# A hybrid encoder block: query latent by rows, later rotary angles, norm scales per token, and a new order at the last two norms

## The chip, the cores and the metric

The kernel runs on one core of one Trainium2 chip. The metric is the device time of one execution in microseconds, given as the median of several runs. One more execution is recorded by the hardware profiler; all the views below come from it.

The engines are named as the profile names them: PE multiplies matrices (PEld are its weight loads), DVE is the vector engine, ACT the scalar engine, POOL the GpSimd engine, SP the engine that issues most transfers. A "q" behind the name (SPq, ACTq) is the engine's own queue, which issues transfers. Every engine takes its instructions in the order in which they stand in its queue.

## The reference

The reference computes one layer for 256 tokens of 2048 features, all in float32:

```python
u = rms_norm(h, norm_pre_mix)
q_sb, k_sb, v_sb, q_lat, kv_lat, k_r, gate_logits = split(u @ w_in)
y_sb  = stick_breaking_attention(q_sb, k_sb, v_sb) @ w_o_sb          # 8 heads of 128
q     = rms_norm(q_lat, q_norm) @ w_uq                               # latent of 768
kv    = rms_norm(kv_lat, kv_norm) @ w_ukv                            # latent of 512
y_mla = mla_attention(q_nope, rope(q_rope), k_nope, rope(k_r), v) @ w_o_mla
g_sb, g_mla = sigmoid(gate_logits + b_gate)
h = h + rms_norm((g_sb * y_sb + g_mla * y_mla) @ w_out, norm_post_mix)
g, up = split(rms_norm(h, norm_pre_ffn) @ w_gate_up)                 # 5632 each
h = h + rms_norm((silu(g) * up) @ w_down, norm_post_ffn)
```

`rms_norm(x, g)` is x times the reciprocal root of its mean square over the features, times g. `rope` turns pairs of features by angles position x frequency; the positions are large (up to some 262,000), so the angle has to be reduced exactly before its sine is taken.

## The kernel before

**Products.** PE works with operands in a rounded float32 format. To keep float32 precision, each operand is split in two: `hi`, the rounded value, made on ACT, and `lo`, the rest, made on DVE. A product is then hi x hi + lo x hi + hi x lo. The activations are split once; the weights, nearly all of the 260 MB that are read, come once from memory and split on the way. One weight unit is a tile of 128 x 1024 (512 KB): SP issues its transfer into `raw`, ACT writes `hi` (L101), DVE writes `lo` (L102), and PE uses both. There are four buffers each of raw, hi and lo, so the splits can be up to four units ahead of PE.

**Stages, in order.** Feature-major products give features on the partitions and tokens along the free axis (`pair`): of the 512 columns of `xs[:, k]` the first 256 are hi of x, the others lo, so a weight tile's hi takes a 512-column product (L164) and its lo a 256-column one (L166); `fold` later adds the two halves. Token-major products (`token`, `two_products`) have 128 tokens on the partitions. The stages are: query latent (`lat_q`, three pairs of 128 features), key/value latent (`lat_kv`, two pairs), rope key (`kr`), `q_sb`, the products from the latents (`qn`, `qr`, `kn`, `vm`), `k_sb` and `v_sb` with the two attentions threaded in between, gates, the two output projections (`wo`), `wout`, the FFN's first product `gu` in eleven column blocks, and `wd`.

**The query latent before.** Each pair runs over all sixteen row tiles of x (four units of four row tiles) before the next pair starts. So the first pair takes x in as it goes: `load_first` loads and splits x's tiles between the cuts of the first four units (L115 on ACT, L116 on DVE).

**Hooks.** Small work is hung on weight units: `at_unit(u, fn)` runs `fn` when unit u's products have been written into the program. There its PE instructions are ordered behind that unit's last product, its ACT and DVE instructions behind the last split. The library's planner settles each engine's order, by its own costs, when the program is built; the engines then follow it. So a hook's product that waits for DVE holds up everything on PE behind it.

- `x_stats`: sums of squares of x, squares on ACT (L231), adds on POOL (L233), at units 3 to 11. `x_scale` (unit 18) makes from them the scale r0 of the first norm, once as a row over the tokens on all partitions (`row_sums`: a product with ones, L132) and once per token as a column (`col_sums`, L138).
- `angles`: the exact range reduction as a chain of some fifty DVE operations of 128 x 256 in eight steps, at units 5 to 12 (the last two of the ten hooks have nothing left).
- `lat_scale`: the scales of the two latents from their sums of squares (adds on POOL, L337 to L340), as rows for q and kv and a column for kv, at units 25, 29 and 32. `rsqrt` is a root on ACT and five operations on DVE; a row has 128 x 256 elements, a column 128 x 2.
- `take_k` and `rope_k`: the rope key's fold and rotation, at units 23 and 26.

**The last two norms.** `wout3` keeps its last four units apart by token half, so half 0 ends before half 1. `after_mix` (called at each half's end) takes squares (ACT), a reciprocal root (`neg_rsqrt`) and then four `residual`s of 128 x 512 on DVE (L721). `turned(t, n)` transposes one of them on PE (four transposes, L727), copies it on ACT (L730) and subtracts on DVE (L731) to get gu's operand `hs`. `gu0` runs its first six row tiles (HEAD0) for half 0, then for half 1, and the dictionary `turns` says before which product which turn is issued. Its first four weight units (AHEAD) are split by halves of 512 columns into slots of their own (L766, L767), written in the program behind the norm's work.

After `wd3`, `finish` does the same for the last norm: for each half the squares, the root, then out = fo x r3 + residual in four parts. Part 3 goes over ACT (L820) and POOL (L821) and is sent from ACT's queue, parts 0 to 2 over DVE (L823) and SP.

Of the kernel before, what the change touches and what calls it, by code (L numbers as in the profile page):

```python
# [10 lines left out]
F32 = mybir.dt.float32  # L11
# [6 lines left out]
P = 128  # L18
# [35 lines left out]
def block_kernel(ctx: ExitStack, tc: tile.TileContext, a: dict, out: bass.AP):  # L54
# [33 lines left out]
    def unit(stream, cols_n, cuts=1, first=None):  # L88
# [7 lines left out]
        for c in range(cuts):  # L96
            cs = slice(c * w, c * w + w)
            if first:
                first(c)
# [30 lines left out]
    def row_sums(acc, name):  # L130
        ps = at_bank(f"{name}_row")
        TE.matmul(ps[:, :T], lhsT=ones, rhs=acc, start=True, stop=True)  # L132
        return ps[:, :T]

    def col_sums(acc, name):
# [4 lines left out]
        return ps[:, 0:2]  # L140

# [12 lines left out]
    def pair(name, stream, K, per, rhs, first=None):  # L154
        ps = mm_pair(f"{name}_ps")
        for u in range(K // per):
            cuts = (4 if u == 0 else 2) if first else 1
            hi, lo = unit(stream, per * 2 * P, cuts, first and (lambda c: first(u, c)))
# [53 lines left out]
    def load_first(u, c):  # L212
        if u == 0:
            load_x(c, 1)
        else:
            load_x(4 * u + 2 * c, 2)

    r0 = const.tile([P, T], F32, tag="r", name="r0")
    r0c = const.tile([P, 2], F32, tag="r0c", name="r0c")
    r0q_krr, r0_sq, trig = slot("r0q_krr"), slot("r0_sq"), slot("trig")  # L220
# [18 lines left out]
    def x_scale():  # L239
        acc = acc_x[0]  # L240
        v = slot("vx")[:, 0]
# [3 lines left out]
        V.tensor_scalar(vc, col_sums(acc, "x"), 1.0 / D, EPS, op0=ALU.mult, op1=ALU.add)  # L245
        rsqrt(r0c, vc)
        V.tensor_tensor(r0_sq[:, 0], r0, r0, op=ALU.mult)
        V.tensor_tensor(r0c_sq, r0c, r0c, op=ALU.mult)
        V.tensor_scalar_mul(r0q, r0, SB_SCALE)
# [75 lines left out]
    lat = {}  # L325
    for nm, n in (("q", 6), ("kv", 4)):
        acc = slot(f"acc_{nm}")[:, 0]
        g = cols[f"{nm}_norm"]
        for p in range(n // 2):
            first = nm == "q" and p == 0  # L330
            ps = pair(f"lat_{nm}{p}", "w_lat", KD, 4, xk, load_first if first else None)
            s = tmp.tile([P, 2, T], F32, tag="t2", name="s", bufs=6)
            fold(ps, None, s)
# [14 lines left out]
        lat[nm] = acc  # L348

# [26 lines left out]
    at_unit(count[0] + 1, take_k)  # L376
# [26 lines left out]
    at_unit(26, rope_k)  # L403
# [4 lines left out]
    def lat_scale(r, sums, acc, r_x, r_x_sq, n, name, scale=None):  # L408
        v = slot(f"v_{name}").rearrange("p a b -> p (a b)")[:, :r.free_size()]
# [499 lines left out]
```

## Time and profile before

| | us |
|---|---|
| runs shown: median (lowest to highest) | 1394.03 (1393.38 to 1395.98) |
| the profiled execution's own time | 1395.33 |
| its span, first to last instruction | 1393.6 |
| first product of `lat_q` | 4.69 |
| first of `lat_kv`, of `kr`, of `q_sb` | 46.70, 70.81, 76.45 |
| first of `gate`, of `wo`, of `wout` | 278.37, 468.09, 558.03 |
| first of `gu`, of `wd` | 648.87, 1143.77 |
| end of the last product | 1384.48 |

How to read the lines of the profile: a line of the timeline has start, duration, engine, line of the kernel, operation, output<-inputs, shapes, and in brackets the idle time of the engine before it and what ended it. A line of groups ends in "| busy us, mean ns of one | idle time before, by what ended it". A line of the waits has the total in us, the number of waits and the longest one. A product's duration is longer than the time to the next one's start, as products overlap on PE; its cost in a row of them is from start to start. A true float32 product (not the rounded format) appears as two instructions.

### The profile page before, as it was taken

What the parts mean: (1) busy time and instruction counts of PE and PEld (TensorE: products, weight loads), DVE (VectorE), ACT (ScalarE), POOL (GpSimd) and SP (SyncE); (2) the same over time, 40 slices, a digit from 0 to 9 for tenths busy, and PEclk for the clock granted to TensorE, in tenths of its full rate; (3) what the DMA queues carried; (4) which work ended last, traced back from release to release, by engine and by line L of the source; (5) the groups of instructions that cost most, each with busy time, mean ns of one, the idle gap of its engine ahead of it and who ended that gap; (6) DMA issues with size and microseconds to landing.
All of it is one profiled execution on the core that took longest, in us unless ns stands there. A gap on an engine that the chain in (4) does not pass through costs nothing.

```text
span 1393.6 us, 16788 instructions
## 1 busy us (share of the span) xinstructions
PE 1373.6 (99%) x6400; PEld 1141.1 (82%) x6400; DVE 804.1 (58%) x927; ACT 681.1 (49%) x816; POOL 59.2 (4%) x89
## 2 busy tenths in 40 slices
PE   7999999999999999999999999999999999999997
PEld 6888888888888888887888888888888888888886
DVE  7997966555555566557555545555455555444444
ACT  7564454466548443445644444444444454434343
POOL 3210000000002100000000000000000001000001
PEclk9999999999999999999999999999999999999999
DMA  7565655455567766664766666665656666666663
GB/s 239 186 207 164 199 167 166 153 182 183 172 209 250 219 184 190 185 196 121 218 190 184 192 186 193 184 191 185 195 185 192 184 207 205 192 196 195 195 188 116
DMA packets 74977, 262.88 MB, mean 189 GB/s; under 512 B 8592, under 2 KB 9744, under 8 KB 74768
## 3 DMA queue, kind: packets, MB, share of 16 engines
q1 hardware_dynamic: 72720, 254.86, 58.8%
q0 software_dynamic: 1744, 6.29, 1.4%
q8 instruction: 50, 0.82, 0.2%
q10 hardware_dynamic: 432, 0.66, 0.1%
q14 instruction: 31, 0.25, 0.0%
HBM read 259.68 MB, written 2.10 MB: 188 GB/s over the span
## 4 chain that ended last, share of the span: by engine, by line
PE 94%; DVE 3%; DMA 1%; ACT 1%; issue 1%; SPq 0%; POOL 0%; DVEq 0%; ACTq 0%
PE gu_ps L629 11%; PE gu_ps L631 11%; PE gu_ps L630 11%; PE wd_ps L200 6%; PE wd_ps L202 6%; PE wd_ps L201 6%; PE gate_ps L202 4%; PE gate_ps L200 4%; PE gate_ps L201 4%; PE k_sb_ps L164 2%; PE q_sb_ps L164 2%; PE wout_ps L200 2%; PE wout_ps L202 2%; PE wo_ps L631 2%; PE wo_ps L630 2%; PE wo_ps L629 2%
## 5 line engine op out<-in xcount | busy, mean ns | idle before, releaser
L773 DVE SCALAR_TENSOR_TENSOR lo_w_gu<-raw_w_gu,packed,hi_w_gu 128x1024 fp32r<-128x1024 f32 x172 | 221.0, 1285 | 213.3 <-ACT hi_w_gu L772 211.6
L772 ACT ACTIVATE hi_w_gu<-raw_w_gu,packed 128x1024 fp32r<-128x1024 f32 x172 | 198.0, 1152 | 230.4 <-PE gu_ps L630 226.4
L629 PE MATMUL gu_ps<-hi_w_gu,hs 128*128 128x512 f32 x704 | 276.6, 393 | 0.9 <-ACT hi_w_gu L766 0.9
L631 PE MATMUL gu_ps<-lo_w_gu,hs 128*128 128x512 f32 x704 | 275.1, 391 | 0.7 <-DVE lo_w_gu L767 0.7
L630 PE MATMUL gu_ps<-hi_w_gu,hs 128*128 128x512 f32 x704 | 273.5, 389 | 0.0
L102 DVE TENSOR_TENSOR lo_w_down<-raw_w_down,hi_w_down 128x1024 fp32r<-128x1024 f32 x88 | 109.2, 1242 | 120.4 <-ACT hi_w_down L101 120.1
L101 ACT ACTIVATE hi_w_down<-raw_w_down 128x1024 fp32r<-128x1024 f32 x88 | 93.3, 1061 | 135.6 <-PE wd_ps L201 127.4
L629 PEld LDWEIGHTS gu_ps<-hi_w_gu,hs 128*128 128x128 f32 x704 | 132.2, 188 | 31.2 <-ACT hi_w_gu L766 2.3
L631 PEld LDWEIGHTS gu_ps<-lo_w_gu,hs 128*128 128x128 f32 x704 | 132.1, 188 | 28.7 <-DVE lo_w_gu L767 1.4
L630 PEld LDWEIGHTS gu_ps<-hi_w_gu,hs 128*128 128x128 f32 x704 | 132.2, 188 | 27.1
L102 DVE TENSOR_TENSOR lo_w_gate<-raw_w_gate,hi_w_gate 128x1024 fp32r<-128x1024 f32 x64 | 78.7, 1234 | 70.1 <-ACT hi_w_gate L101 63.8
L200 PE MATMUL gate_ps<-hi_w_gate,xs 128*128 128x512 f32 x256 | 100.6, 393 | 0.0
L202 PE MATMUL gate_ps<-lo_w_gate,xs 128*128 128x512 f32 x256 | 99.7, 390 | 0.0
L201 PE MATMUL gate_ps<-hi_w_gate,xs 128*128 128x512 f32 x256 | 99.6, 389 | 0.0
L101 ACT ACTIVATE hi_w_gate<-raw_w_gate 128x1024 fp32r<-128x1024 f32 x64 | 67.4, 1055 | 62.0 <-PE gate_ps L201 53.7
L102 DVE TENSOR_TENSOR lo_w_out<-raw_w_out,hi_w_out 128x1024 fp32r<-128x1024 f32 x32 | 39.2, 1226 | 38.8 <-ACT hi_w_out L101 38.6
L101 ACT ACTIVATE hi_w_o<-raw_w_o 128x1024 fp32r<-128x1024 f32 x32 | 34.0, 1061 | 51.7 <-PE wo_ps L630 45.2
L102 DVE TENSOR_TENSOR lo_w_o<-raw_w_o,hi_w_o 128x1024 fp32r<-128x1024 f32 x32 | 39.2, 1225 | 32.0 <-ACT hi_w_o L101 31.4
L101 ACT ACTIVATE hi_w_out<-raw_w_out 128x1024 fp32r<-128x1024 f32 x32 | 34.0, 1061 | 47.2 <-PE wout_ps L201 36.3
L202 PEld LDWEIGHTS gate_ps<-lo_w_gate,xs 128*128 128x128 f32 x256 | 48.0, 188 | 10.1
L201 PEld LDWEIGHTS gate_ps<-hi_w_gate,xs 128*128 128x128 f32 x256 | 48.1, 188 | 9.7
L200 PEld LDWEIGHTS gate_ps<-hi_w_gate,xs 128*128 128x128 f32 x256 | 48.1, 188 | 9.6
(447 smaller groups left out, 2557.0 us busy)
## 6 DMA issues: line engine op xcount, KB each, us to landing
raw_w_gu<-in_w_gu SPq DMA_DIRECT2D x176, 512.0 KB, 3.6
raw_w_down<-in_w_down SPq DMA_DIRECT2D x88, 512.0 KB, 3.5
raw_w_gate<-in_w_gate SPq DMA_DIRECT2D x64, 512.0 KB, 3.6
raw_w_o<-in_w_o SPq DMA_DIRECT2D x32, 512.0 KB, 3.8
raw_w_out<-in_w_out SPq DMA_DIRECT2D x32, 512.0 KB, 3.5
raw_w_lat<-in_w_lat SPq DMA_DIRECT2D x16, 512.0 KB, 4.8
raw_w_q<-in_w_q SPq DMA_DIRECT2D x16, 512.0 KB, 4.0
raw_w_k<-in_w_k SPq DMA_DIRECT2D x16, 512.0 KB, 3.8
```

Of the source, the lines that this page charges most:

```text
L101: split_ins[0] = S.activation(hi[:, cs], raw[:, cs], AF.Copy)
L102: split_ins[1] = V.tensor_tensor(lo[:, cs], raw[:, cs], hi[:, cs].bitcast(F32), op=ALU.subtract)
L164: TE.matmul(ps[:, j, :], lhsT=hi[:, o:o + P], rhs=r, start=k == 0, stop=False, skip_group_check=True)
L200: TE.matmul(ps[t], lhsT=l[0][:, ts], rhs=hi[:, cs], start=k == 0, stop=False)
L201: TE.matmul(ps[t], lhsT=l[1][:, ts], rhs=hi[:, cs], start=False, stop=False)
L202: mm = TE.matmul(ps[t], lhsT=l[0][:, ts], rhs=lo[:, cs], start=False, stop=k == K - 1)
L629: TE.matmul(ps[t][:, j], lhsT=x[0][:, ts], rhs=hi[j], start=k == 0, stop=False)
L630: TE.matmul(ps[t][:, j], lhsT=x[1][:, ts], rhs=hi[j], start=False, stop=False)
L631: mm = TE.matmul(ps[t][:, j], lhsT=x[0][:, ts], rhs=lo[j], start=False, stop=k == K - 1)
L772: split_ins[0] = S.activation(hi, raw, AF.Copy, scale=g)
L773: split_ins[1] = V.scalar_tensor_tensor(lo, raw, g, hi.bitcast(F32), op0=ALU.mult, op1=ALU.subtract)
```

## The change

- **Query latent.** The weight stream of the query latent is laid out by rows: one unit is one row tile with all 768 columns (sixteen units of 384 KB instead of twelve of 512 KB), and the three pairs are computed side by side in six accumulators, the row tile outermost. x's tiles are loaded one by one (from the fifth on two by two) ahead of the unit that needs them. The first two units are cut in three. The last two row tiles are run pair by pair, so that the pairs end one after the other. Units are numbered anew: four more lie ahead of everything behind the query latent.
- **Angles.** The same eight steps at units 17, 19, 21, 24, 26, 28, 31 and 32 (ten hooks again). The statistics of x are at units 2 to 17; `rope_k` is at unit 40.
- **Scales.** All three are made per token as columns of two; `spread` multiplies the ones matrix by each column (DVE) and, at a later unit, turns it into a row by a product with the identity (PE), copied out on ACT. x's sums are at unit 22 with the spread at 26, q's at 27 and 33, kv's at 30 and 36. `row_sums` is gone.
- **Norm before the FFN.** gu0's first four weight units are issued at units 11, 14, 19 and 22 of the 24 of wout0 to wout2. `after_mix` issues two residuals per half, and `later_residuals` the other four behind the turn (1, 0). The turns stand in a new order. The FFN's squares on ACT come behind the second half's root.
- **Last norm.** POOL has no part in it. For half 0 all four parts go over DVE and SP. For half 1, part 3 is made on PE: the identity times the residual plus a diagonal of r3 times fo, copied out on ACT and sent from ACT's queue.

```diff
+    def spread(col, name, u, *rows):
+        b = const.tile([P, 2, P], F32, tag="spread", name=f"{name}_b", bufs=2)
+        for t in range(2):
+            V.tensor_scalar_mul(b[:, t], ones, col[:, t:t + 1])
+        def rest():
+            ps = at_bank(f"{name}_row")
+            for t in range(2):
+                TE.matmul(ps[:, t * P:t * P + P], lhsT=b[:, t], rhs=ident, start=t == 0, stop=True, ...)
+            for row, factor in rows:
+                S.activation(row, ps[:, :T], AF.Copy, scale=factor)
+        at_unit(u, rest)
...
     def x_scale():
-        V.tensor_scalar(v, row_sums(acc, "x"), 1.0 / D, EPS, op0=ALU.mult, op1=ALU.add)
-        rsqrt(r0, v)
...
+        spread(r0c, "r0", 26, (r0, 1.0), (r0q, SB_SCALE))
...
-    for u in range(3, 12):
+    for u in [*range(2, 17, 2), 17]:
         at_unit(u, lambda: next(stat_steps, None))
-    at_unit(18, x_scale)
-    for u in [*range(5, 14), 16]:
+    at_unit(22, x_scale)
+    for u in (17, 19, 21, 24, 26, 28, 31, 32, 34, 37):
         at_unit(u, lambda: next(trig_steps, None))
...
+    def first_products():
+        both = [mm_pair(f"lat_q{p}_ps") for p in range(2)]
+        ps = [[b[:, j] for j in range(2)] for b in both] + [[at_bank(f"lat_q2{j}_ps") for j in range(2)]]
+        order = [(k, p) for k in range(KD - 2) for p in range(3)]
+        order += [(k, p) for p in range(3) for k in range(KD - 2, KD)]
+        w = {}
+        for k, p in order:
+            if k not in w:
+                if k < 4:
+                    load_x(k, 1)
+                elif k % 2 == 0:
+                    load_x(k, 2)
+                w[k] = unit("w_lat", 768, 3 if k < 2 else 1)
+            hi, lo = w[k]
+            for j in range(2):
+                o = (2 * p + j) * P
+                TE.matmul(ps[p][j], lhsT=hi[:, o:o + P], rhs=xs[:, k], ...)
+                mm = TE.matmul(ps[p][j][:, 0:T], lhsT=lo[:, o:o + P], rhs=xs[:, k, 0], ...)
+            if p == 2:
+                unit_done(mm)
+            if k == KD - 1:
+                yield ps[p]
...
-    at_unit(25, lambda: lat_scale(rq, row_sums, lat["q"], r0, r0_sq[:, 0], 768, "q", MLA_SCALE))
-    at_unit(29, lambda: lat_scale(rkv, row_sums, lat["kv"], r0, r0_sq[:, 0], 512, "kv"))
-    at_unit(32, lambda: lat_scale(rkvc, col_sums, lat["kv"], r0c, r0c_sq, 512, "kvc"))
+    at_unit(27, lambda: lat_scale(rqc, "q", 768, 33, rq, MLA_SCALE))
+    at_unit(30, lambda: lat_scale(rkvc, "kv", 512, 36, rkv, 1.0))
...
     def after_mix(ps, t):
         squares(ss1, ps, t, 3)
         r1s[t] = neg_rsqrt(ss1, t, "r1", lambda: mg_part(ps, t, 3))
+        roots.append(ready[0][0])
         with tc.issue_after(ready[0][1]):
-            for n in range(4):
+            for n in range(2):
                 residual(t, n)
...
+    def later_residuals():
+        with tc.issue_after(last_turn[0]):
+            for n in range(2, 4):
+                for t in range(2):
+                    residual(t, n)
...
+    for k in range(AHEAD):
+        at_unit(count[0] + (11, 14, 19, 22)[k], lambda k=k: first_units.update({k: up_unit(0, k)}))
...
     def ffn_squares(t):
-        for n in range(4):
-            squares(ss2, hres[t, n], t, n)
+        with tc.issue_after(roots[1]):
+            for n in range(4):
+                squares(ss2, hres[t, n], t, n)
...
+        with tc.issue_after(first_residual[k >= HEAD0]):
+            return up_unit(c, k)
...
-    turns = {(0, 0): (1,), (0, 2): (2,), (0, 4): (3,), (1, 0): (0, 1), (1, 3): (2,), (1, 6): (3,)}
+    steps = {(0, 0): [(turned, 0, 1)], (0, 5): [(turned, 1, 0), (later_residuals,)], (1, 0): [(turned, 1, 1)],
+             (1, 2): [(turned, 0, 2)], (1, 3): [(turned, 1, 2)], (1, 4): [(turned, 0, 3)], (1, 5): [(turned, 1, 3)]}
...
     def finish(ps, t):
         squares(ss3, ps, t, 3)
+        if t == 1:
+            last = at_bank("last")
+            TE.matmul(last, lhsT=ident, rhs=hres[t, 3], start=True, stop=False)
         r3 = neg_rsqrt(ss3, t, "r3", lambda: fo_part(ps, t, 3))
-        for n in (3, 0, 1, 2):
+        if t == 1:
+            diag = const.tile([P, P], F32, tag="diag", name="diag")
+            V.tensor_scalar_mul(diag, ident, r3)
+            TE.matmul(last, lhsT=diag, rhs=fo[t, 3], start=False, stop=True)
+        for n in range(4):
             o = fo[t, n]
-            if n == 3:
-                S.activation(o, o, AF.Copy, scale=r3)
-                G.tensor_tensor(o, o, hres[t, n], op=ALU.add)
+            if t == 1 and n == 3:
+                S.activation(o, last, AF.Copy)
             else:
                 V.scalar_tensor_tensor(o, o, r3, hres[t, n], op0=ALU.mult, op1=ALU.add)
-            (S if n == 3 else nc.sync).dma_start(out[...], o)
+            (S if t == 1 and n == 3 else nc.sync).dma_start(out[...], o)
```

More of the change, by code (lines that the diff above doesn't have):

```diff
@@ L152, in unit_done, with pair @@
                 fn()
[L154 removed]
+    def pair(name, stream, K, per, rhs):
         ps = mm_pair(f"{name}_ps")
         for u in range(K // per):
[L157 to L158 removed]
+            hi, lo = unit(stream, per * 2 * P)
             for i in range(per):
```

108 lines of the change are left out of this document (57 added, 51 removed).

## The prediction

> **What bounds the kernel now.** I read the page's busy shares first, then PE's waits, then the timelines of the three places where PE isn't back to back: the start, the turn from the output projection to the FFN, and the tail.
>
> ```profile
> span 1393.6 us, 16788 instructions
> PE 1373.6 (99%) x6400; PEld 1141.1 (82%) x6400; DVE 804.1 (58%) x927; ACT 681.1 (49%) x816; POOL 59.2 (4%) x89
> ```
>
> PE is the bound, so only idle or slow PE time can be won; the change leaves the big products alone. PE's waits name the places:
>
> ```profile
> PE lat_q_ps L164 <- DVE xs L116: 4.7, 1, 4.7
> PE lat_q_ps L166 <- DVE lo_w_lat L102: 2.6, 5, 1.0
> PE lat_q_ps L164 <- ACT hi_w_lat L101: 1.2, 1, 1.2
> PE gu_ps L629 <- ACT hi_w_gu L766: 0.9, 2, 0.7
> PE gu_ps L631 <- DVE lo_w_gu L767: 0.7, 2, 0.4
> PE lat_kv_ps L166 <- DVE lo_w_lat L102: 0.4, 1, 0.4
> ```
>
> The 4.7 us are the first load; the next two rows (3.8 us) lie in the query latent, two in gu0, one in the key/value latent.
>
> **Part 1, query latent by rows.** PE's timeline, start to start:
>
> ```profile
> 4.69 0.77 PE L164 MATMUL lat_q_ps<-xs,hi_w_lat 128*128 128x512 f32 x1 [4.69 <-DVE xs L116]
> 6.11 0.63 PE L164 MATMUL lat_q_ps<-xs,hi_w_lat 128*128 128x512 f32 x1
> 6.75 0.63 PE L164 MATMUL lat_q_ps<-xs,hi_w_lat 128*128 128x512 f32 x1
> 11.68 0.50 PE L164 MATMUL lat_q_ps<-xs,hi_w_lat 128*128 128x512 f32 x1 [1.16 <-ACT hi_w_lat L101]
> 46.70 0.40 PE L164 MATMUL lat_kv_ps<-xs,hi_w_lat 128*128 128x512 f32 x1
> 47.05 0.40 PE L164 MATMUL lat_kv_ps<-xs,hi_w_lat 128*128 128x512 f32 x1
> ```
>
> A hi/lo pair takes 0.64 us early (6.11 to 6.75) and 0.35 later (46.70 to 47.05), though the granted clock of the windows below reads 1.00 in both. The 96 pairs of the query latent need 96 x 0.35 = 33.6; they took 46.70 - 4.69 = 42.0. So 8.4 us go to the slow start and the stalls. Before, the first quarter of the pairs needs all sixteen row tiles of x; now row tile k brings six pairs, 2.1 us of PE, for one x tile and one weight tile of 768 columns. When are these there?
>
> ```profile
> 8.37 0.42 ACT L101 ACTIVATE hi_w_lat<-raw_w_lat 128x256 fp32r<-128x256 f32 x1 [0.83 <-DMA raw_w_lat<-in_w_lat]
> 10.99 0.63 ACT L101 ACTIVATE hi_w_lat<-raw_w_lat 128x512 fp32r<-128x512 f32 x1 [1.02 <-DMA raw_w_lat<-in_w_lat]
> 8.00:11.00 3.00, 2.52 (x8) 1.36 (x6) 1.36 (x4) 1.33 (x4) 0.00 (x0) 1.00 0.81 224
> 11.00:14.00 3.00, 2.10 (x10) 1.52 (x11) 2.17 (x4) 2.49 (x6) 0.00 (x0) 1.00 0.99 343
> L101 ACT ACTIVATE hi_w_uqn<-raw_w_uqn 128x768 fp32r<-128x768 f32 x8 | 6.8, 847 | 10.9 <-PE q_sb_ps L164 5.7 <-PE qn_ps L164 4.0 <-issue 1.2
> L102 DVE TENSOR_TENSOR lo_w_uqn<-raw_w_uqn,hi_w_uqn 128x768 fp32r<-128x768 f32 x8 | 7.7, 957 | 7.4 <-ACT hi_w_uqn L101 7.4
> ```
>
> The windows' last columns are the granted clock, DMA share and GB/s. Before, eight 128 KB pieces had landed at 8.37 and 1.57 MB at 10.99. The new order also starts with eight 128 KB pieces (tiles 0 and 1), so PE starts at 4.69 as now; tile 2 completes 1.57 MB: at 10.99 at the latest, or 8.37 + 0.52 MB at 343 GB/s = 9.9 with its longer rows. Splitting 768 columns costs 0.85 + 0.96, so tile 2 can run at 11.7 to 12.8; I take 12.2. PE's first twelve pairs end near then: slow up to about 11 (the change of pace lies before 11.68), (11 - 4.69) / 0.64 = 9.9 pairs, and 2.1 more at 0.35 reach 11.7. Then 14 tiles x 6 x 0.351 = 29.5: the latent ends at 41.7 instead of 46.70, 5.0 less. Later tiles need 0.52 MB in 2.1 us, 249 GB/s, under the 343; DVE per tile is 0.96 + 0.48, ACT no more. One late tile more would cost 1 us: 4.9 won, 3.5 to 5.5.
>
> The rows show 343 GB/s with 256 KB transfers, several in flight. The Trainium skill (DMA: Bandwidth & Descriptors, section Bandwidth) asks for transfers of 1 MiB and gives 0.68 us for 4 KB and 6.15 for 1 MB. An estimate from that page, one transfer after the other, makes 4.1 us of a 384 KB and a 128 KB piece, and this part a loss of some 20 us; the trace speaks against it, and the sum goes by the trace.
>
> **Part 2, angles and scales.** The angles move from units 5 to 13 (in the query latent) to 17 to 37, behind it; the latents' folds of q now come in one lump there; the three 256-wide rsqrt chains become two-column ones.
>
> ```profile
> 47.00:79.00 32.00, 30.96 (x62) 1.00 0.55 165
> L345 DVE SCALAR_TENSOR_TENSOR lat_q<-s,packed,lat_q 128x256 fp32r<-128x256 f32 x6 | 5.6, 948 | 0.2 <-ACT lat_q L344 0.2
> L345 DVE SCALAR_TENSOR_TENSOR lat_kv<-s,packed,lat_kv 128x256 fp32r<-128x256 f32 x4 | 1.8, 480 | 0.0
> L124 DVE RECIPROCAL r<-r 128x256 f32<-128x256 f32 x1 | 1.8, 1754 | 0.0
> 42.91 4.36 POOL L233 TENSOR_TENSOR ssx<-ssx,sq 128x512 f32<-128x512 f32 x3
> ```
>
> The first row is DVE alone, busy and its count: 30.96 of 32 us. DVE is full where PE hardly waits yet, so here the gain can be given back. The stretch from 47 to 79 (key/value latent, rope key, first unit of q_sb) keeps its PE work. Its DVE work changes by: the row chain out, about 1.75 + three ops like the 0.4 us ones, -2.9; folds of two more q pairs, each one 0.6 us operation and two of the 0.48 row, which overlap to 1.4, +2.8; the angles, 9.2 before and 9.6 now by their ops of 0.28 and 0.42; and more adds on POOL beside it, some six more of about 0.9. An add slows DVE: 0.95 instead of 0.48 in the rows; half of their 5.7 us is +2.9, bounds 0 and 5.7. Together +3.2. Against it stand two units split ahead (2 x 1.2), as DVE has 2.1 us per 1.44 of work in the new query latent. Net +0.8 on PE, from -0.4 (today's wait goes too) to +3.6.
>
> PE also gets three spread products and one column product more in place of three row products. A row product is 0.43 (67.16 to 67.59) and two 128-column products of the same type are as long; the added column product is 67.59 to 67.95 and a slower restart: 0.45.
>
> ```profile
> 67.16 0.59 PE L132 MATMUL x_row<-ssx,ones 128*128 128x256 f32 x2
> 67.59 0.50 PE L138 MATMUL x_col<-ones,ssx 128*128 128x1 f32 x4
> 67.95 0.47 PE L164 MATMUL lat_kv_ps<-xs,hi_w_lat 128*128 128x512 f32 x1
> 82.73 0.15 DVE L248 TENSOR_TENSOR r0c_sq<-r0c 128x2 f32<-128x2 f32 x1
> ```
>
> A new wait: PE, in order, stands at unit 26 for the spread operand that DVE makes from r0c. Before, r0c took 82.73 - 67.95 = 14.8 from the sums, 2.9 of it the row chain's; now units 23 to 26 give it 4 x 2.8 + 0.4 = 11.7. It just fits: 0, at most 3, and it is the same backlog as above. Behind it would stand q_sb's products. Units 27 to 33 and 30 to 36 leave six units, 17 us: nothing. Angles and rope_k land by unit 40, needed after 50. Part 2 costs 0.8 + 0.45 = 1.25.
>
> **Part 3, gu0.** Four weight units are now loaded and split between units of wout1 and wout2, where ACT and DVE have room; only two residuals of each half come before the first turn.
>
> ```profile
> 644.91 0.60 PE L727 MATMUL tp<-ident,x 128*128 128x128 f32 x4
> 645.26 0.48 PE L200 MATMUL wout_ps<-hi_w_out,mixed3h 128*128 128x512 f32 x1
> 646.74 1.47 PE L727 MATMUL tp<-ident,x 128*128 128x128 f32 x12
> 648.87 0.50 PE L629 MATMUL gu_ps<-hi_w_gu,hs 128*128 128x512 f32 x1 [0.65 <-ACT hi_w_gu L766]
> 662.62 0.50 PE L629 MATMUL gu_ps<-hi_w_gu,hs 128*128 128x512 f32 x1
> 650.51 2.73 DVE L721 SCALAR_TENSOR_TENSOR x<-mg,r,x 128x512 f32<-128x512 f32 x4
> ```
>
> From 646.74 to 662.62, 15.9 us, PE does 28 transposes and 39 products. (The stretch's groups count 14, 13 and 12 products by line, the first of the next three among them and one unrecorded.) A clean group of four transposes takes 0.35 (644.91 to 645.26) and some 0.1 of restart (that product lasts 0.48, one in mid-stream 0.39); a product is 0.227 after the one before it (three in 0.68). So 7 x 0.45 + 39 x 0.227 = 12.0, and 3.9 can be won. What is late next is the second half's residual, 650.51 to 653.2 for all four and near 652 for the two that now come first, against its turn on PE at 646.74 + 0.45 + 5 x 6 x 0.227 = 654.0; the four late residuals follow (4 x 0.68) and the first of their turns stands on PE at 658.6, two units into the second half. If four splits in wout cost PE something, it is the 12 products of a unit (2.7 us) against DVE's 1.23 + 1.48: level, with four buffers of lead. I take 3.4, 2.0 to 3.9.
>
> **Part 4, tail.**
>
> ```profile
> 1384.09 0.39 PE L202 MATMUL wd_ps<-lo_w_down,hid10h 128*128 128x512 f32 x1
> 1384.56 0.35 ACTq L824 DMA_DIRECT2D out_h<-fin  x1
> 1384.96 0.60 ACT L687 ACTIVATE sqo<-wd_ps 128x512 f32<-128x512 f32 x1 [2.27 <-POOL fin L821]
> 1387.04 3.08 DVE L823 SCALAR_TENSOR_TENSOR fin<-fin,r,x 128x512 f32<-128x512 f32 x3
> 1387.84 1.73 POOL L821 TENSOR_TENSOR fin<-fin,x 128x512 f32<-128x512 f32 x1 [3.31 <-ACT fin L820]
> ```
>
> PE ends at 1384.48, but ACT's queue holds the squares behind an output transfer that waits for POOL: 0.45 lost. Without POOL the three last DVE products take 3 x 0.68 (the residuals' row, the same instruction) = 2.05, not 3.08; the diagonal, 128 wide, lies between the 0.15 of a two-column operation and the 0.48 of a 256-wide one: 0.2, ahead of them. Gain 0.45 + 1.0 - 0.2 = 1.25. The fourth part goes over PE (0.86, twice a 256-column product of that type), ACT (0.6, the squares' shape) and ACT's queue, ready beside the third. The opening product of that pair, on the residual, lies in the 2.5 us that r3 takes. Two output transfers closer together cost some 0.15. 1.1, from 0.6 to 1.6.
>
> **Sum.** -4.9 + 1.25 - 3.4 - 1.1 = -8.2 (bounds: -10 to -3). The profiled execution took 1395.33 (span 1393.6), 1.3 over the median 1394.03 of the runs; 1387.1 by the one, 1385.8 by the other. Medians are compared: 1386.
>
> **Rivals.**
> - DVE takes the start back (+4.9 instead of +0.8 in units 17 to 28): for it, DVE at 97%; against it, 0.4 us of waits there now. 1390.
> - gu0 is bound by the residuals and turns, not by the weights: part 3 gives 0.5. For it, ACT makes the turns' copies between the splits; against it, both named waits are on w_gu. 1389. Both rivals at once: 1393, no change.
> - Slower: each POOL add holds DVE for its whole 1.45 us (4.36 / 3) in units 17 to 26. That is 11.1 us of adds instead of the 2.9 counted, 8.2 more, and r0c's chain, behind that, makes PE wait its 3 us at the spread: -8.2 + 8.2 + 3.1 = +3.1, 1397. It decides from 11 us of backlog. Against it: 0.95, not 1.9, for L345.
>
> The Trainium skill (SBUF — State Buffer, section Who interferes with whom) says that a DVE instruction with two SBUF inputs and a GpSimd one that reads SBUF fully block each other, the later waiting; by that rule the last rival, 1397. The trace shows only part of such waits.
>
> **Chances.** Forecast 0.62 (own range 1383 to 1389), DVE 0.14, gu0 0.10, both 0.06, slower 0.08. Under 0.2% (2.8 us) a measurement can't tell from no change. Faster: 0.62 + 0.10 + most of 0.14 = 0.83; same 0.09; slower 0.08. The range 1382 to 1391 leaves out the last two cases and some edges.
>
> **What would show it.** Right: the key/value latent starts near 42; its span stays within 24 to 25 us; no PE wait at the spread; gu0's first product within 1 us of wout's last, with no wait on w_gu, and its first 39 products over in 12 to 13 us; the last squares within 0.1 us of PE's end and no POOL in the tail. Wrong: waits of PE on lo_w_lat, lo_w_kr, lo_w_q or the spread operand over 3 us in all; waits on the turned rows in gu0; slower products anywhere else.

## The result and the profile after

| | before | after |
|---|---|---|
| median of the runs side by side (lowest to highest) | 1394.32 (1393.38 to 1395.98) | 1387.47 (1386.74 to 1387.83) |
| the profiled execution, its span | 1395.33, 1393.6 | 1387.83, 1386.1 |
| first product of the key/value latent, of `kr`, of `q_sb` | 46.70, 70.81, 76.45 | 42.42, 65.47, 71.14 |
| first product behind `q_sb` (q/k norms) | 122.81 | 119.88 |
| last product of `wout`, first of `gu` | 646.51, 648.87 | 643.82, 644.41 |
| first product of `wd`, last of `wd`, end | 1143.77, 1384.09, 1393.60 | 1137.06, 1377.38, 1386.13 |

The ratio is 0.9949, with a 95% interval of 0.9932 to 0.9966: 6.9 us faster by the medians, 7.5 by the two spans. The forecast was 1386.0. Cut at the stages of the table, the spans' 7.5 us come from: query latent -4.4 (and 0.1 later at the start); from there to the end of `q_sb`, +1.35; small shifts over attention, gate and wo, +0.2; turn to the FFN, -4.0; tail, -0.8.

The waits of PE in the changed kernel (engine, tile and line, what ended the wait; total, count, longest):

```profile
PE lat_q_ps L342 <- DVE xs L114: 4.8, 1, 4.8
PE last L878 <- DVE diag L877: 1.6, 1, 1.6
PE lat_q_ps L342 <- ACT hi_w_lat L99: 1.3, 1, 1.3
PE r_row L144 <- DVE r_b L139: 1.2, 1, 1.2
PE lat_q_ps L343 <- DVE lo_w_lat L100: 0.5, 1, 0.5
```

The first load stays. The five waits on `lo_w_lat` in the query latent have become one pair of waits at one tile; `w_gu` is gone from the list. New are the wait at the spread, which the prediction had put at nothing, and one in the tail. The timeline of PE shows where these stand:

```profile
10.36 0.28 PE L343 MATMUL lat_q_ps<-xs,lo_w_lat 128*128 128x256 f32 x1
11.91 0.50 PE L342 MATMUL lat_q_ps<-xs,hi_w_lat 128*128 128x512 f32 x1 [1.27 <-ACT hi_w_lat L99]
12.91 0.39 PE L343 MATMUL lat_q_ps<-xs,lo_w_lat 128*128 128x256 f32 x1 [0.49 <-DVE lo_w_lat L100]
...
42.42 0.40 PE L172 MATMUL lat_kv_ps<-xs,hi_w_lat 128*128 128x512 f32 x1
...
75.28 0.71 PE L144 MATMUL r_row<-ident,r_b 128*128 128x128 f32 x4 [1.16 <-DVE r_b L139]
...
643.82 0.40 PE L210 MATMUL wout_ps<-lo_w_out,mixed3h 128*128 128x512 f32 x1
644.06 0.60 PE L759 MATMUL tp<-ident,x 128*128 128x128 f32 x4
644.41 0.48 PE L659 MATMUL gu_ps<-hi_w_gu,hs 128*128 128x512 f32 x1
...
654.55 0.39 PE L659 MATMUL gu_ps<-hi_w_gu,hs 128*128 128x512 f32 x1
```

PE has used up row tiles 0 and 1 by 10.6 and stands until tile 2 is split (hi at 11.9, lo a second later); from 12.91 to 42.42 it is not interrupted again, 29.5 us for 14 tiles. The first product of the FFN comes 0.6 us behind wout's last, with four transposes between, where it was 2.4 before; the last row is gu's fortieth product, which before started 8.4 us later:

```profile
662.95 0.40 PE L630 MATMUL gu_ps<-hi_w_gu,hs 128*128 128x512 f32 x1
```

The tail, all engines:

```profile
1377.38 0.40 PE L210 MATMUL wd_ps<-lo_w_down,hid10h 128*128 128x512 f32 x1
1377.82 0.60 ACT L717 ACTIVATE sqo<-wd_ps 128x512 f32<-128x512 f32 x1 [3.25 <-PE wd_ps L210]
...
1379.90 0.28 DVE L877 TENSOR_SCALAR diag<-ident,r 128x128 f32<-128x128 f32 x1
1380.11 2.07 DVE L884 SCALAR_TENSOR_TENSOR fin<-fin,r,x 128x512 f32<-128x512 f32 x3
1380.24 1.12 PE L878 MATMUL last<-fin,diag 128*128 128x512 f32 x2 [1.61 <-DVE diag L877]
1381.41 0.60 ACT L882 ACTIVATE fin<-last 128x512 f32<-128x512 f32 x1 [2.42 <-PE last L878]
1382.03 0.35 ACTq L885 DMA_DIRECT2D out_h<-fin  x1
```

The squares start when PE ends, POOL is gone, and DVE's three parts take 2.07 instead of 3.08. The part that goes over PE is ready (1382.0) when DVE's third is (1382.2).

### The profile page after: what moved, and what is told of

Its sections match the earlier page's. It is cut to its first block, busy times and chain, and to the rows that moved or that the text cites. A ratio compares the mean times of both kernels' runs of the same rounds, so it can differ in the third digit from the quotient of the medians.

```text
span 1386.1 us, 16822 instructions
## 1 busy us (share of the span) xinstructions
PE 1371.9 (99%) x6414; PEld 1142.2 (82%) x6414; DVE 794.2 (57%) x923; ACT 680.4 (49%) x821; POOL 58.5 (4%) x87
## 4 chain that ended last, share of the span: by engine, by line
PE 96%; DVE 3%; DMA 0%; issue 0%; SPq 0%; ACT 0%; DVEq 0%
PE gu_ps L659 12%; PE gu_ps L660 12%; PE gu_ps L661 12%; PE wd_ps L208 6%; PE wd_ps L210 6%; PE wd_ps L209 6%; PE gate_ps L208 4%; PE gate_ps L210 4%; PE gate_ps L209 4%; PE k_sb_ps L172 2%; PE wout_ps L208 2%; PE wo_ps L661 2%; PE wo_ps L659 2%; PE wout_ps L210 2%; PE wout_ps L209 2%; PE wo_ps L660 2%
```

## The experiments

Each was profiled in one execution beside the kernel before on the same chip, except the last two, which were timed over five rounds. The single times of the changed kernel lie within 0.75 us of their median, and the start of the key/value latent differs between runs of one code: 41.4 to 42.4 in the traces here with the changed query latent as it is, 46.0 to 46.7 in the three with the old one. So each part is read from its own stage of the trace.

### The tail alone

The kernel before with the new `finish` and nothing else.

```diff
-                S.activation(o, o, AF.Copy, scale=r3)
-                G.tensor_tensor(o, o, hres[t, n], op=ALU.add)
+                S.activation(o, last, AF.Copy)      # part 3 of half 1, from PE
```

> The kernel before with the new finish of the last norm alone. If the parts stand by themselves: no stage up to the last product of wd moves by more than 0.2 us, and from the start of that product to the end of the span it takes 8.7 to 8.8 us, as in the changed kernel, instead of 9.5: 0.8 us in all. If the tail's gain leans on something earlier in the change (the place of the residuals, another table load), the stretch stays at 9.3 or more.

Measured: 1393.49; from the last product to the end 8.89 us, 0.62 less than the 9.51 before and a little over the 8.8 expected. The stages ahead, whose code is the same, moved by more than the 0.2 us expected: the query latent took 0.31 less and the stretch from `wout`'s last product to `wd` 496.78 instead of 497.26. Two executions of one code differ by that much there. Short of the forecast 1.1 here too, so the difference belongs to this part and not to what runs ahead of it.

### The turn to the FFN alone

The kernel before with the hunks of part 3 (early first units, two residuals first, new order of turns).

```diff
+        at_unit(count[0] + (11, 14, 19, 22)[k], lambda k=k: first_units.update({k: up_unit(0, k)}))
-            for n in range(4):
+            for n in range(2):
                 residual(t, n)
```

> The kernel before with the new order at the norm ahead of the FFN alone (early weight units, two residuals first, turns in the new order). If the parts stand by themselves: from the start of wout's last product to the start of wd it takes 493.2 us as in the changed kernel, 4.0 less than before (497.3), and nothing before it moves. If the changed kernel's 4.0 depend on what came earlier (slots or buffers freed sooner), less than 3 is found.

Measured: 1390.4; from wout's last product to the first of `wd` 493.24 us, as in the changed kernel (497.26 before). The part is worth 4.0 us by itself (3.5 against the 496.78 of the run above) and needs none of the others.

### The first units of gu late again

The changed kernel, but with the first four weight units loaded and split where their products stand.

```diff
-    for k in range(AHEAD):
-        at_unit(count[0] + (11, 14, 19, 22)[k], lambda k=k: first_units.update({k: up_unit(0, k)}))
```

> The changed kernel with gu0's first four weight units issued in their place again, so behind the norm's first residuals; residuals and turns in the new order. Theory (the weights' late splits were what gu0 waited for): 2.5 to 3.5 of the 4.0 us are lost again, with waits of PE on hi or lo of w_gu. Rival (the new order of residuals and turns is what pays): under 1 us is lost.

Measured: 1389.84; the same stretch takes 496.15 us. PE's waits show why:

```profile
PE gu_ps L659 <- ACT hi_w_gu L788: 1.5, 1, 1.5
PE gu_ps L661 <- DVE lo_w_gu L789: 0.4, 1, 0.4
```

2.9 of the 4.0 us hang on the early weights, the other 1.1 (0.6 against the 496.78) on the order of the residuals and turns. Of the 2.9 the two rows name 1.9; the rest was not traced to a row.

### The angles early again

The changed kernel with the angle steps at units 5 to 13 and 16, as before the change.

```diff
-    for u in (17, 19, 21, 24, 26, 28, 31, 32, 34, 37):
+    for u in (5, 6, 7, 8, 9, 10, 11, 12, 13, 16):
         at_unit(u, lambda: next(trig_steps, None))
```

> The changed kernel with the angle steps back at units 5 to 13 and 16, so in the query latent; all else stays. Theory (the vector engine had room in the new query latent, some 5 of 22 us idle between 21 and 43, and the move behind it was not needed for the gain): the key/value latent still starts within 0.7 us of 42.4, the wait for the spread operand of r0 falls from 1.2 to under 0.4, as 3 us of angle operations no longer stand between the links of the r0c chain; span 1385 to 1386. Rival (rows outermost only pays with the angles out of the way): the adds on POOL and the angles together make lo tiles late, the key/value latent starts 2 to 5 us later, span 1388 to 1390.

Measured: 1408.1, and the key/value latent starts at 64.15. Both theories miss by 16 us or more. The waits of all engines over the first 70 us:

```profile
PE lat_q_ps L342 <- DVE xs L114: 24.2, 3, 12.9
...
ACT xs L113 <- DMA xT<-in_xT: 12.0, 6, 4.5
```

PE waits for x, not for weights. In the program's order on SP's queue the last five of x's loads had moved behind weight loads, and those wait for a raw buffer that DVE has still to free (the load of tiles 6 and 7 comes behind six more weight loads than in the changed kernel; the last two of x's loads lie behind four of the key/value latent's weights). So this run does not tell whether DVE had room; that needed SP's order held fixed, the next one.

### The angles early, x's loads kept in place

As the one above, with each weight unit of the query latent issued behind the load of x that is written last ahead of it.

```diff
+                with tc.issue_after(x_dma[-1].ins):
                     w[k] = unit("w_lat", 768, 3 if k < 2 else 1)
```

> Computes the same as the changed kernel. The angle steps are asked for at units 5 to 13 and 16 again, and each weight unit of the query latent may be issued only behind the last load of x, so that SP's queue keeps x's loads in the places that they have in the changed kernel. Theory (DVE has no room for the angles in the query latent: it is idle for 38.2 - 28.9 = 9.3 us there in the changed kernel, and the angles' instructions are 17.7 us of busy time): PE waits for lo_w_lat or x in the query latent for 3 us or more beyond the changed kernel, the kv latent starts at 45.5 to 48, a part of it comes back because the stretch up to the q/k norms has no angles in it: 1388.5 to 1391.5. Rival (in the run with early angles only the loads of x were in the wrong place, DVE has room): the kv latent starts within 1 us of 42.4 and the wait before r_row is gone: 1386 to 1387.

Measured: 1403.05; the key/value latent starts at 58.96. The rival falls; the theory has the direction, and a third of the size at most. The windows (PE, PEld, DVE, ACT, POOL busy; granted clock, DMA share, GB/s), then the waits over the first 70 us:

```profile
20.00:40.00 20.00, 13.74 (x64) 10.29 (x62) 19.59 (x42) 8.55 (x13) 6.43 (x3) 0.91 0.49 154
40.00:59.00 19.00, 12.96 (x60) 10.38 (x60) 15.29 (x34) 7.66 (x13) 0.00 (x0) 0.82 0.47 159
```

```profile
ACT trig L311 <- DVE turn L309: 7.9, 1, 7.9
...
PE lat_q_ps L345 <- ACT trig L312: 5.5, 1, 5.5
```

From 20 to 40 DVE is busy for 19.6 of the 20 us while PE works 13.7: the angles and the splits don't fit there together. What the theory's sum left out is order. The engines take their work in the order written: the sine stands in ACT's queue ahead of weight splits and waits 7.9 us for the angle chain on DVE. PE's longest wait is put down to the sine too, as that ended last before it, but the timeline speaks for another:

```profile
47.00 0.87 DVE L116 SCALAR_TENSOR_TENSOR xs<-xT,packed,xs 128x256 fp32r<-128x256 f32 x2
47.44 0.83 ACT L99 ACTIVATE hi_w_lat<-raw_w_lat 128x768 fp32r<-128x768 f32 x1
47.62 1.19 PE L345 MATMUL lat_q_ps<-xs,hi_w_lat 128*128 128x512 f32 x2 [5.46 <-ACT trig L312]
```

PE's product, the first of row tile 12, starts while the split behind the sine still runs, so it does not need that one. It starts 0.15 us after DVE has written the lo half of x's tile 12 (the first of the two in the first row, to 47.48); that stood behind the angle chain in DVE's own queue, while ACT had made the hi half by 32.3. The wait of 3.5 us that ends at 23.93 follows DVE's split of x's tile 6 by 0.14 us in the same way. From 4.8 to 60 us DVE is not even full (44.8 of 55.2 us). After its stops PE was slower too: the granted clock reads 0.91 and 0.82 in the two windows. So with the angles at these units part 1 is lost, and moving them out was needed; other places in the query latent were not tried. Idle time summed over a stage was not a measure of what fits into it.

### The angles behind the spread operand

The spread's wait of 1.2 us was the step that the prediction had at nothing. DVE and POOL around it in the changed kernel:

```profile
59.60 0.91 POOL L366 TENSOR_TENSOR acc_kv<-sq 128x256 f32<-128x256 f32 x1 [2.63 <-ACT sq L364]
...
65.04 0.15 DVE L243 TENSOR_SCALAR vxc<-x_col 128x2 f32<-128x2 f32 x1
...
71.32 0.17 DVE L125 TENSOR_SCALAR newton<-newton 128x2 f32<-128x2 f32 x1
71.39 1.23 DVE L100 TENSOR_TENSOR lo_w_q<-raw_w_q,hi_w_q 128x1024 fp32r<-128x1024 f32 x1
71.95 1.48 POOL L368 TENSOR_TENSOR acc_kv<-acc_kv,sq 128x256 f32<-128x256 f32 x1 [11.44 <-ACT sq L364]
...
72.73 0.72 DVE L126 TENSOR_TENSOR r0c<-r0c,newton 128x2 f32<-128x2 f32 x1
...
73.51 1.27 POOL L369 TENSOR_TENSOR acc_kv<-acc_kv,sq 128x256 f32<-128x256 f32 x1
74.10 0.69 DVE L245 TENSOR_TENSOR r0c_sq<-r0c 128x2 f32<-128x2 f32 x1
74.72 0.57 DVE L139 TENSOR_SCALAR r_b<-ones,r0c 128x128 f32<-128x128 f32 x2
```

A chain of nine small operations takes 10.2 us, from 65.04 to 75.29. Two causes are visible: other work stands between its links in DVE's queue, which has no idle time here, and its last links run beside POOL's additions and take 0.7 us instead of 0.16. One kernel was made against each. The first allows angle steps 2 to 10 on DVE only behind the spread operand:

```diff
+    def trig_step():
+        with tc.issue_after(spread_b["r0"]):
+            next(trig_steps, None)
+    at_unit(17, lambda: next(trig_steps, None))
+    for u in (23, 24, 25, 26, 28, 31, 32, 34, 37):
+        at_unit(u, trig_step)
```

> Computes the same as the changed kernel. Angle steps 2 to 10 may now only be issued on DVE behind the two multiplies that write the spread operand (L139 in the changed kernel); nine angle instructions of 0.2 to 0.34 us (2.5 us), one split (1.15 us) and one fold (0.6 us) so leave the stretch between the scale's variance (L243, at 65.0) and those multiplies (at 74.7). Theory (the spread is late because its chain of small DVE instructions shares a full DVE queue with the angles): the spread operand is ready by about 71 and PE's wait of 1.2 us before r_row is gone; kr to the q/k norms is 1.0 to 1.3 us shorter than in the changed kernel, about 1386.4 us. Rival (the links are slow because of POOL's two adds at 71.9 to 74.8): the chain still ends only 1 us earlier at most where it meets the adds, a wait of over 0.5 us stays. Second rival (the stretch up to the q/k norms is bounded by DVE's sum, so the wait only moves to a weight split): the wait before r_row goes and one of 0.5 us or more on lo_w_q or kraw comes; 1387.5.

Measured: 1385.83. DVE:

```profile
64.78 0.15 DVE L122 RECIPROCAL r0c<-r0c 128x2 f32<-128x2 f32 x1
65.84 0.47 DVE L141 TENSOR_SCALAR r_b<-ones,r0c 128x128 f32<-128x128 f32 x2
...
70.90 0.97 DVE L381 SCALAR_TENSOR_TENSOR lat_kv<-s,packed,lat_kv 128x256 fp32r<-128x256 f32 x1
71.79 0.95 DVE L299 TENSOR_TENSOR turn<-turn,pr 128x256 f32<-128x256 f32 x1
```

The operand is there at 66.3, 9 us earlier (8.3 counted from `q_sb`'s first product), and no wait is left at the spread (PE's only wait of the first 125 us is the first load). The stretch from `q_sb`'s first product to the q/k norms is 1.47 us shorter (47.27 instead of 48.74). POOL's additions still run, at 70.2 to 72.5, and now slow two operations (0.97 and 0.95 instead of some 0.45) that nobody waits for. Nothing new waits behind the moved angles.

### The key/value latent without its second pair of additions

The second: POOL's two additions at 71.9 to 74.8 left out, DVE's order the same.

```diff
-            else:
+            elif nm == "q":
                 G.tensor_tensor(acc, acc, sq[:, 0], op=ALU.add)
                 G.tensor_tensor(acc, acc, sq[:, 1], op=ALU.add)
```

> Leaves out two POOL additions of 256 columns: the sum of squares behind the kv latent's norm has only the first half of its terms, all else is as in the changed kernel and DVE's order is the same. Theory (POOL's adds at 71.9 to 74.8 stretch the last links of the scale's chain: L126 0.72 where L125 took 0.17, L245 0.69, the two multiplies 0.57 each): those links take 0.16 to 0.25 each and the wait before r_row falls from 1.2 to 0.2 us or less; about 1386.5 us. Rival (the order of DVE's full queue makes it late, POOL is only beside it): the links keep 0.5 us or more or the wait stays at 0.8 us or more; 1387.5.

Measured: 1386.64. DVE and PE:

```profile
72.64 0.15 DVE L126 TENSOR_TENSOR r0c<-r0c,newton 128x2 f32<-128x2 f32 x1
73.44 0.15 DVE L245 TENSOR_TENSOR r0c_sq<-r0c 128x2 f32<-128x2 f32 x1
73.51 0.47 DVE L139 TENSOR_SCALAR r_b<-ones,r0c 128x128 f32<-128x128 f32 x2
```

```profile
73.83 0.71 PE L144 MATMUL r_row<-ident,r_b 128*128 128x128 f32 x4 [0.33 <-DVE r_b L139]
```

The links take 0.15 us, the operand comes 0.7 us earlier counted from `q_sb`'s first product, and PE waits 0.33 instead of 1.16, between the 0.2 of the theory and the 0.8 of the rival. So both causes are real, and either cure helps: the additions made 0.8 us of the wait, and the 0.3 that stays without them is left to the queue's order, whose cure took all of it.

### The query latent's third and fourth tile in pieces

```diff
-                w[k] = unit("w_lat", 768, 3 if k < 2 else 1)
+                w[k] = unit("w_lat", 768, 3 if k < 4 else 1)
```

> Computes the same as the changed kernel. The third and fourth weight units of the query latent are also loaded and split in three pieces of 256 columns instead of one of 768. Theory (PE's waits of 1.3 and 0.5 us at the third row tile are for the last byte of a 384 KB transfer and its single split): with pieces the first split starts when a third has landed, the two waits fall to 0.6 us or less in all, the kv latent starts 1 us earlier after PE's first product than the 37.6 us of the changed kernel, about 1386.4. Rival (the transfers share one bandwidth, so that the third tile's last piece lands when it did, or later with short rows): the waits stay at 1.5 us or more or come back at the fourth tile; 1387.5 to 1389.

Measured: 1389.41. PE's timeline has no wait left at the third tile and a new one later:

```profile
17.51 0.50 PE L342 MATMUL lat_q_ps<-xs,hi_w_lat 128*128 128x512 f32 x1 [1.57 <-DVE xs L114]
```

The key/value latent starts at 43.05, later than in any other run that has the angles behind the query latent. The rate over the first 20 us is the same (247 and 251 GB/s), but from 8 to 14 us it is lower, 243 and 292 GB/s in the two halves where the changed kernel has 286 and 369. SP issues these pieces one in about 0.47 us, so tile 4's weights were issued at 8.9 instead of 7.0. ACT waited for them until 14.21, x's tile 4 was split behind them, and DVE's part of that took 1.45 us beside an addition on POOL (1.52 in the changed kernel, where it began 0.7 us earlier). What came earlier for tiles 2 and 3 was thus missing for tile 4. That has the rival's sign, a wait that comes back at a later tile. Whether the bytes or the number of transfers bind was not tested.

### The last quarter on DVE

The changed kernel without the two products on PE: all four parts of half 1 go over DVE.

```diff
-        if t == 1:
-            diag = const.tile([P, P], F32, tag="diag", name="diag")
-            V.tensor_scalar_mul(diag, ident, r3)
-            TE.matmul(last, lhsT=diag, rhs=fo[t, 3], start=False, stop=True)
```

> Computes the same as the changed kernel, but the last quarter of rows 128 to 255 is formed on DVE like the other three, without the two products on PE. Theory (the PE path ends as late as DVE's third part, so that it saves less than one DVE instruction of 0.72 us): last product to end 0.3 to 0.6 us longer than the changed kernel's 8.74. Rival (the PE path is worth its whole DVE instruction): 0.7 us or more longer. Second rival (the end is set by the last transfer's landing alone): within 0.15 us.

Measured: 1387.02; last product to end 8.56 us, 0.18 less than with the PE path; all three theories expected the other side or nothing. The outputs' issues show it, each a row with the KB and the time to landing; first the changed kernel's two last (1382.03 and 1382.20), then this kernel's last (1382.04, where the last product began at 1376.76):

```profile
out_h<-fin ACTq DMA_DIRECT2D x1, 256.0 KB, 2.4
out_h<-fin SPq DMA_DIRECT2D x1, 256.0 KB, 2.9
```

```profile
out_h<-fin ACTq DMA_DIRECT2D x1, 256.0 KB, 2.2
```

One output of 256 KB moves in some 0.69 us (both kernels show some 380 GB/s in the full slices of the tail), as long as DVE needs for one part (2.74 / 4 = 0.69). So the transfers can't go faster than DVE feeds them. On the PE path the last two outputs were issued 0.17 us apart and the last landed after 2.9 us; measured from the last product, it landed at 7.7. Without it the last issue is at 5.3 instead of 4.8 and lands at 7.5. Behind the diagonal, which takes 0.21 us, the first transfer was issued at 3.49 instead of 3.29: that is the size of what the PE path cost.

### The changed kernel again, and the two edits together

> The changed kernel itself once more, beside the next one on the same chip. Expected: 1387.4, from 1386.7 to 1387.8, and the start of the kv latent between 41.4 and 42.5.

Measured: 1387.44 (1387.25 to 1388.13), ratio to before 0.9944 (0.993 to 0.9958).

The second kernel has the angles behind the spread operand and the last quarter on DVE (the two diffs above).

> Computes the same as the changed kernel, with two edits of the earlier experiments together: angle steps 2 to 10 behind the spread operand, and the last quarter formed on DVE. Theory (the two are in different places and add): 1.5 us less for the wait of PE and the slow stretch up to the q/k norms, 0.2 us less in the tail: 1385.7, 1.3 to 2.1 us under the changed kernel on the same chip. Rival (the gain of the first was the start of that one run, which differs by about 1 us between runs of one code): within 0.7 us of the changed kernel.

Measured: 1385.65 (1385.22 to 1386.06), ratio to before 0.9931 (0.9918 to 0.9943). It is 1.8 us under the changed kernel on the same chip, and their ranges don't meet. Its trace has 1.47 us less from `q_sb` to the q/k norms than the changed kernel's first trace (1.7 less than its second) and 0.2 less in the tail, the same two numbers as the single edits, so they add. This version beats both kernels.

## Why the prediction was right, point by point

**Sum.** -8.2 was forecast, -7.5 measured between the two spans, -6.9 by the medians; the range and the sign held. The terms, against what each stage shows:

| part | forecast (bounds) | measured |
|---|---|---|
| 1, query latent | -4.9 (-5.5 to -3.5) | -4.4 |
| 2, angles and scales | +1.25 (+0.05 to +4.05) | +1.35 |
| 3, turn to the FFN | -3.4 (-3.9 to -2.0) | -4.0 |
| 4, tail | -1.1 (-1.6 to -0.6) | -0.8 |

**Part 1.** The mechanism held: one stop at tile 2, then 14 tiles at PE's pace of 29.5 us. Tile 2's first half was taken at 11.91, where 12.2 was forecast. The mis-sized term is the split: the sum let the tile's six pairs start once, but its lo half came after hi had been used. From the hi product to the lo product it took 1.00 us instead of 0.23, and 0.3 of these 0.77 had been won at the start of the tile. This half microsecond is that of one execution: over the seven traces with the changed query latent as it is, the stage takes 36.6 to 37.6 us from PE's first product, and the forecast's 37.0 lies within. The step on PE's slow start was wrong and cost nothing: the pace changed at 8.0, not near 11, so PE was through tiles 0 and 1 at 10.6 and only stood longer.

**Part 2.** The size held, the make-up did not. The forecast was 0.8 for DVE's backlog and 0.45 for an added product, with no wait at the spread. From the key/value latent to `q_sb` the backlog cost nothing: that stretch is 1.0 shorter (28.72 instead of 29.75), with no wait of PE on a split. The old wait of 0.4 is gone and the x row product (0.43) has left it; the last 0.2 was not traced. From `q_sb` to the q/k norms it is 2.4 longer: 1.5 of it went when the angles were put behind the spread, the wait and its restart; the other 0.9 stayed and goes with the spread and column products that now stand there (what PE does in that stretch beside `q_sb` takes 2.05 us with the angles behind the spread, 1.09 before). So the sum came right by errors that cancel, -1.0 where +0.8 was put, 0.9 for 0.45 and 1.5 for nothing, and its size was luck. The failed step is "it just fits: 0": the chain was sized by its time before the change less the row chain's, 11.9 us against 11.7. From the end of the sums' products (62.6) to the end of the operand (75.3) it took 12.7, where PE asked for it after 11.5 (74.1, the end of the product before the wait). Of the wait of 1.16 the last links under POOL's additions made 0.8, as the run without these shows, and the other work between the links the rest: what the prediction had spread over DVE's whole backlog mattered at one place only.

**Part 3.** The early weights are 2.9 of 4.0, as the forecast's theory had it; the rival that turns and residuals bind gets the 1.1. The gain lies 0.1 beyond the bound of 3.9, less than the half microsecond by which this stretch differs between two executions of the old code. The bound was also set too low: it took 0.45 us for a group of transposes with its restart, but the products around a group start 0.59 apart in the changed kernel, 0.36 more than in mid-stream, which makes 0.6 us for seven groups. (And the 39 products up to 662.62 are 38: all 2112 products of `gu` are recorded, and that row is the thirty-ninth.) From the first turn behind `wout` to the fortieth product it now takes 10.5 us instead of 16.2, but not all of these 5.7 are won: four of the seven groups of transposes now come behind it, some 1.4 us. The forecast had kept 0.5 back from its bound, and no wait took it.

**Part 4.** The steps on the engines were right: the squares 0.43 earlier (0.45), DVE's three parts 1.0 shorter (1.0), the diagonal 0.21 (0.2): DVE ends 1.23 earlier from the last product (1.25). The mis-sized term is "two output transfers closer together cost some 0.15": the last landed after 2.9 us where the last of before took 2.3, 0.6 of it. The PE path itself, taken as a gain, was a loss of 0.2. The last output before, issued at 1390.15:

```profile
out_h<-fin SPq DMA_DIRECT2D x1, 256.0 KB, 2.3
```

**The signs.** These came out: the key/value latent starts at 42.42, gu's first product 0.6 us behind wout's last with no wait on `w_gu`, the last squares at PE's end, and POOL has no part in the tail. These did not: a wait stood at the spread, the key/value latent's span was 23.05 us and not 24 to 25 (24.11 before), and gu's first 39 products were over in 10.5 us and not 12 to 13, as turns had moved behind them.

**The rivals.** DVE taking the start back did not occur, nor gu0 bound by turns. The slower case asked that each addition holds DVE for all of its 1.45 us. POOL was indeed busy for 11.0 us from the key/value latent to `q_sb` (5.0 before), near the rival's 11.1, and PE lost nothing in that stretch. The rows quoted above show what decides. The link at 72.73 came while the first addition ran and ended with it (73.45, the addition at 73.43), as did the one at 74.10 with the second (74.79 and 74.78): there DVE waited for all that was left of the addition. The split at 71.39 had begun before the addition; it took its usual 1.2, and the addition took 1.48 instead of the 0.91 of the one at 59.60. One operation between them (73.77, two inputs as well) took its usual 0.41 though the second addition is recorded from 73.51; that addition took 1.27 where it takes 0.80 in the kernel with the angles behind the spread, so it reads as held itself. The Trainium skill (SBUF — State Buffer, section Who interferes with whom) says that whoever issues first holds the shared ports for its whole instruction; these rows agree with it, and the prediction's remark that the trace shows only part of such waits was too quick. The rival's price was still too high: about half of the waiting at these two additions fell on POOL, and beside the other additions DVE's half fell on operations that PE did not wait for, as in the kernel with the angles behind the spread (0.97 and 0.95, no wait of PE).

## What to carry to other kernels

A chain of tiny operations in a full in-order queue takes as long as the work between its links: when PE will stand at the chain's end, order the other work behind the chain instead of comparing total times. Idle time summed over a stage does not say that work fits into it; what stands behind a waiting instruction on each engine's queue, SP's loads among them, does. Where a wait can have several causes, compare its end with the end of everything that the instruction reads. At the end of a kernel compare the rate of the output transfers with the rate of what feeds them before taking work off the feeding engine.

## What the runs showed of the hardware

PE's pace at the start changes at another moment in each run of the same code. In the changed kernel's trace a pair of products goes from 0.64 to 0.35 us at 8.0 (rows below), and at 11.1 in the repeated run of the same code, 10.5 with late weights, 9.2 with DVE's tail; before, with gaps in PE's work, not ahead of 11.7. The windows print a granted clock of 1.00 all the time. But the trace's own record of that clock begins only at 7.82 in the first of these runs and at 10.89 in the repeated one, 0.2 us ahead of the change of pace; what lies earlier has no record and is counted as 1.00.

```profile
7.29 0.41 PE L343 MATMUL lat_q_ps<-xs,lo_w_lat 128*128 128x256 f32 x1
7.51 0.55 PE L342 MATMUL lat_q_ps<-xs,hi_w_lat 128*128 128x512 f32 x1
8.01 0.39 PE L342 MATMUL lat_q_ps<-xs,hi_w_lat 128*128 128x512 f32 x1
8.36 0.40 PE L342 MATMUL lat_q_ps<-xs,hi_w_lat 128*128 128x512 f32 x1
```

The Trainium skill (TensorE: Matmul & The Clock Gate, section Part 1: The HAM clock gate) states that the array runs at half its clock until one window of about 3.4 us was busy, and that the windows run freely. From the first product at 4.8 the seven traces with the changed query latent as it is have 3.2 to 6.4 us to the change. A spread of about one window agrees with a phase that the program doesn't set; the least value is 0.2 under the page's 3.4. In the two runs with early angles, where PE stood for long, the recorded stretches of one clock last 3.41, 6.83, 13.65 and 17.07 us, all multiples of 3.41. In this kernel the moment matters little, since tile 2 comes at 11.1 to 11.9 in all seven.
